# Hi and lo parts of the output projection's operand made earlier and kept in DRAM, in a transformer block's fp32 kernel

## The chip, the cores and the metric

The kernel runs on one core of one Trainium2 chip. The metric is the device time of one execution in microseconds. Engines are named as the profile names them: PE (TensorE matmuls), PEld (its weight loads), DVE (VectorE), ACT (ScalarE), POOL (GpSimd) and SP, whose queue issues most loads.

## The reference, cut to what matters

One block over 512 tokens of width 2048. An input projection feeds two mixers; their outputs are joined, projected and added to the residual; a gated feed-forward layer follows. What the change touches is the joint in the middle:

```python
u = rmsnorm(h, attn_norm_w[l])
z, xbc, dt_raw, q, kc, vc, ks, vs, kw, vw, gate_raw = jnp.split(u @ w_in[l], split_at, axis=-1)
y_ssd = ssd_mixer(z, xbc, dt_raw, ...)      # ends in: rmsnorm(y * jax.nn.silu(z), norm_w)
y_att = nsa_mixer(q, kc, vc, ks, vs, kw, vw, gate_raw, ...)
mixed = jnp.concatenate([y_ssd, y_att], axis=-1)
h = h + mixed @ w_out[l]
```

`y_ssd` and `y_att` are 1024 wide each: eight tiles of 128 channels by 512 tokens each. The norm inside `ssd_mixer` runs over all 1024 channels, so it needs all eight gated tiles before any of them is final.

## The kernel before, in words

Every matmul is done in a split form: an operand a is written as hi + lo, two tiles in a format that PE multiplies fast, and a product is hi·hi + hi·lo + lo·hi, three matmuls (lines 234 to 236). The hi part is a copy on ACT (`a_hi`, L125), the lo part a difference on DVE or POOL (`lo`, L128; L972 where a scale is folded in).

The input projection is a list of 41 units, each 128 output channels by 512 tokens over 16 blocks of 128 of the contraction. `run_unit` runs a unit: it takes its weights in groups of four blocks (256 KB by SP into the ring `raw`, four buffers, L200), splits each group into `whi` and `wlo` (rings of four buffers each) up to three groups ahead, and does three matmuls a block with the operand `U` (tile name u), which holds the hi and lo parts of 16 blocks. All other work is written as Python generators that a small scheduler `sch` steps: each block of a unit is one tick, and a generator says after how many ticks it wants to go on. A unit's result is taken from PSUM by its generator (`ev_...`), and a unit starts only when the one two before it has been taken.

The order of the units is written out by hand: the dt/gates unit, B, C and X of the SSD mixer, the compressed keys, z0 to z3, and then four attention groups g = 0 to 3, each with VS (selected/window values), KS (keys) and two query units, with the z blocks 4 to 7 set between them: z4 and z5 before group 1, z6 before group 2, z7 before group 3. Attention itself is a generator that runs beside the projection and goes on beside the output projection; when the input projection is over, groups 0 and 1 (four tiles of 128 channels) are finished.

`ev_z` makes a gated tile: DVE scales, ACT gates, POOL multiplies by y (read back from DRAM), the tile goes to `gy_d` in DRAM by POOL's queue (L570), its squares are summed in `acc2`, and after z7 `rms_stats` makes the row `row2` of the norm's factors (flag "r2"). A finished attention tile goes to `at_d` (L896) while the operand `U` is still in use, and after that directly into `U`.

The last unit of the input projection is the second query unit of group 3. Ahead of it `pre_ms` starts `ms_in`, which fills blocks 0 to 7 of `U` with the SSD operand: SP loads a tile of `gy_d` into the ring `raw` (L969), POOL multiplies it by `row2`, ACT makes the hi part with the norm's weight folded in, DVE the lo part (L972). Ahead of the first unit of the output projection `pre_out` starts `ma_in`, which does the like for the attention tiles that are ready: SP loads a tile of `at_d` (L985) into the place of the lo part, ACT makes hi, DVE makes lo in place. The first units of the output projection use blocks 0 to 10 or 11 of the operand (the lists `NS`), the rest is added in a later pass.

The compiler layer under the kernel puts the instructions of every engine in an order by a modelled timeline, so the order on an engine is not that of the program text; for PE alone, from the output projection on, it is that of the text (`manual_schedule`). A buffer of a ring is reused when those who read it are done, a store to DRAM among them.

Of the kernel before, what the change touches and what calls it, by code (L numbers as in the profile page):

```python
# [8 lines left out]
F32 = mybir.dt.float32  # L9
F32R = mybir.dt.float32r  # L10
AF = mybir.ActivationFunctionType
ALU = mybir.AluOpType
# [24 lines left out]
C_AN, C_FN, C_LN, C_SN, C_CW, C_CB, C_PE, C_W2 = 0, 16, 32, 48, 56, 104, 116, 148  # L37
# [78 lines left out]
def body(ctx, tc, xT, w_in, w_out, w_gate, w_up, w_down, w1k, w1v, cols, rows, kst, out):  # L116
    nc = tc.nc
    act, dve, pool, pe = nc.scalar, nc.vector, nc.gpsimd, nc.tensor
    sch = Sched()

    def f(ap):
        return ap.bitcast(F32)

    def a_hi(dst, src, scale=1.0):
        act.activation(dst, src, AF.Copy, scale=scale)  # L125

    def lo(eng, dst, src, hi):
        eng.tensor_tensor(dst, src, f(hi), ALU.subtract)  # L128
# [4 lines left out]
    def mul(eng, o, a, b):  # L133
        eng.tensor_tensor(o, a, b, ALU.mult)  # L134

    def add(eng, o, a, b):
        eng.tensor_tensor(o, a, b, ALU.add)  # L137
# [4 lines left out]
    dram = ctx.enter_context(tc.tile_pool(name="dram", bufs=1, space=bass.MemoryType.DRAM))  # L142
# [9 lines left out]
    def ps_t():  # L152
        return ps("t", 2)

    def ps_v():
        return ps("v", 1)

    def ps_m():
        return ps("m", 1)

    gy_d = dram.tile([8, 128, 512], F32, name="gy_d")
    y_d = dram.tile([4, 128, 512], F32, name="y_d")
    at_d = dram.tile([8, 128, 512], F32, name="at_d")
    h1_d = dram.tile([KD, 128, 512], F32, name="h1_d")
    h_d = dram.tile([NJ, 128, 4, 256], F32, name="h_d")
    g_d = dram.tile([NP, 7, 128, 512], F32, name="g_d")
# [3 lines left out]
    def open_pool(name, stack=None, **kw):  # L170
        es = ExitStack()
        pools[name] = (es, es.enter_context(tc.tile_pool(name=name, bufs=1, reuse_waits="tile", **kw)))
        return pools[name][1]
# [19 lines left out]
    raw, hi_t, lo_t = {}, {}, {}  # L193
# [78 lines left out]
    def col(c, n=1):  # L272
        return colc[:, c:c + n]
# [4 lines left out]
    def rms_stats(acc, n, dst, flag, gap=4):  # L278
        nb = acc.shape[1] // 128
        p = ps_m()  # L280
        for i in range(nb):
            pe.matmul(p[:, i:i + 1], acc[:, i * 128:(i + 1) * 128], ones[:, 0:1], start=True, stop=True)
        dve.tensor_scalar(rst[:, 0:nb], p[:, 0:nb], 1.0 / n, EPS, op0=ALU.mult, op1=ALU.add)
        r = rst[:, 4:4 + nb]
        pool.tensor_tensor(r, rst[:, 0:nb], nhalf[:, 0:nb], ALU.pow)
        yield gap
        p = ps_m()
        for i in range(nb):
            pe.transpose(p[:, i * 128:(i + 1) * 128], r[:, i:i + 1].to_broadcast([128, 128]), ident)
        act.activation(dst, p[:, 0:128 * nb], AF.Copy)  # L290
        sch.flags.add(flag)
# [7 lines left out]
    U = up.tile([128, 2, KD, 512], F32R, name="u")  # L299
    wp = open_pool("wp", side="right")  # L300
# [247 lines left out]
    def ev_z(t):  # L548
        def ev(p):
            yield from sch.wait("r1", ("y", t // 4))  # L550
            g, j = divmod(t, 4)
            if g == 0:
                sp = pools["ssd"][1]
                zs = sp.tile([128, 512], F32, tag="zs", name="zs", bufs=2)
                mul(dve, zs, p, rrow)
                act.activation(zs, zs, AF.Silu)
                q = ps_m()
                for i in range(4):
                    pe.transpose(q[:, i * 128:(i + 1) * 128], R["y", g][:, i, j * 128:(j + 1) * 128], ident)
                mul(dve, zs, q, zs)  # L560
            else:
                yield from sch.wait("att")
                sp = pools["att"][1]
                y = sp.tile([128, 512], F32, tag="yz", name="yz", bufs=1)
                nc.sync.dma_start(y, y_d[j])
                zs = sp.tile([128, 512], F32, tag="qs", name="zs", bufs=2)
                mul(dve, zs, p, rrow)
                act.activation(zs, zs, AF.Silu)
                mul(pool, zs, zs, y)
            nc.gpsimd.dma_start(gy_d[t], zs)  # L570
            if t == 0:
                act.activation(acc2, zs, AF.Square)
            else:
                sq = sp.tile([128, 512], F32, tag="sq" if g == 0 else "yz", name="sq", bufs=1)
                act.activation(sq, zs, AF.Square)
                add(pool, acc2, acc2, sq)
            sch.flags.add(("gy", t))
            if t == 7:
                P2["row2"] = sp.tile([128, 512], F32, tag="yz", name="row2", bufs=1)
                sch.add(rms_stats(acc2, 1024, P2["row2"], "r2"))  # L580
        return ev

    P2 = {}

    def ev_kc(g):
        def ev(p):
# [200 lines left out]
    def attention():  # L787
# [6 lines left out]
        for g in range(4):  # L794
# [22 lines left out]
            p = ps_t()  # L817
# [51 lines left out]
            def pvmm(h, br):  # L869
                th, tl = pt.pop((h, br))  # L870
                if br == 0:
                    o = po[h] = ps_v()
                    pe.matmul(o, vpad[:, h, :], ch, start=True, stop=False)
                    pe.matmul(o, vpad[:, h, :], cl, start=False, stop=False)
                o = po[h]
                for kb in range(4):
                    for t in (th, tl):
                        rhs = t[:, 4 * kb:3 * kb + 4, :].rearrange("p a b -> p (a b)")
                        pe.matmul(o[:, kb * 128:512], v[:, kb, br, :], rhs, start=False,
                                  stop=(br == 1 and kb == 3 and t is tl))  # L880
                if br == 1:
                    if h % 2 == 0:
                        R["at"] = ap.tile([128, 512], F32, tag="at", name="at", bufs=1)
                    at = R["at"]
                    a, b = (0, 64) if h % 2 == 0 else (64, 0)
                    fo = ap.tile([128, 512], F32, tag="fo", name="fo", bufs=1)
                    act.activation(fo[a:a + 64, :], o[b:b + 64, :], AF.Copy)
                    add(dve, at[a:a + 64, :], o[a:a + 64, :], fo[a:a + 64, :])
                    if h % 2:
                        k = 2 * g + h // 2  # L890
                        if "ma" in P2:
                            h_, l_ = P2["ma"][k]
                            a_hi(h_, at)
                            lo(dve, l_, at, h_)
                        else:
                            nc.gpsimd.dma_start(at_d[k], at)  # L896
                            P2["at"] = k
                        sch.flags.add(("at", k))

            n = len(items)  # L900
            for s in range(n + LAG + 1):
# [7 lines left out]
                if s < n:  # L909
                    norm(*items[s])  # L910
                yield P2.get("pace", PACE)[s % len(PACE)]
                if 0 <= s - LAG - 1 < n and items[s - LAG - 1][2] == 3:
# [38 lines left out]
        order += [U_B[g], U_C[g]] + U_X[g]  # L951
    order += U_KC + U_Z[0:4]
    for g in range(4):
        z = {0: [], 1: [4, 5], 2: [6], 3: [7]}[g]
        order += [U_Z[t] for t in z] + [U_VS[g], U_KS[g]] + U_Q[g]
    units = [Unit(win(u), KD, u_rhs, ev[u], pre=pre_att if u == U_VS[0] else (lambda: pre_ms()) if u == order[-1] else None) for u in order]


    def pre_ms():
        P2["ms"] = [(U[:, 0, k], U[:, 1, k]) for k in range(8)]  # L960
        sch.add(ms_in())

    def ms_in():
        assert "r2" in sch.flags
        for k in range(8):
            yield 2
            h_, l_ = P2["ms"][k]
            t = wp.tile([128, 512], F32, tag="raw", name="gy", bufs=4)
            nc.sync.dma_start(t, gy_d[k])  # L969
            mul(pool, t, t, P2["row2"])  # L970
            a_hi(h_, t, scale=col(C_SN + k))
            dve.scalar_tensor_tensor(l_, t, col(C_SN + k), f(h_), op0=ALU.mult, op1=ALU.subtract)  # L972
            sch.flags.add(("ms", k))

    def pre_out():
# [5 lines left out]
    def ma_in(n):  # L981

        for k in range(n):
            h_, l_ = P2["ma"][k]
            nc.sync.dma_start(f(l_), at_d[k])  # L985
            yield 1 if k < 4 else 8
            a_hi(h_, f(l_))
            lo(dve, l_, f(l_), h_)
            sch.flags.add(("ma", k))

    def ev_os(c):
        def ev(p):
            if c >= 12:
                t = wp.tile([128, 512], F32, tag="raw", name="h1", bufs=4)
            else:
                t = pools["att"][1].tile([128, 512], F32, tag="yz", name="h1", bufs=1)
            act.activation(t, p, AF.Copy)
            nc.gpsimd.dma_start(t, xT[c], accum_op=ALU.add)
            yield 4
            nc.gpsimd.dma_start(h1_d[c], t)  # L1000
        return ev
# [720 lines left out]
    for v, (j, a, b) in enumerate(visits):  # L1722
# [14 lines left out]
        for n, p in enumerate(SEQ_D):  # L1737
            blk, sums = q["form"][p]
            if n == 0 and v in (2, 4):
                later[5 + (v == 4)] = len(items)  # L1740
            s = Step(blk, g_rhs(p, a), bk(p), after=af(p),
                     before=down_before(v, n) if n < 2 and v < NJ - 1 else None, sums=sums)
# [30 lines left out]
    for k in range(KD):  # L1773
        if k % 4 == 0:
            issue_split(k // 4)
        t = xt[:, k, :]
# [5 lines left out]
    for k in range(KD):  # L1782
        t = xt[:, k, :]
# [125 lines left out]
```

## Time and profile before

| | |
|---|---|
| median of 3 runs | 2241.39 us (2238.38 to 2245.98) |
| the profiled execution | 2243.56 us, span 2241.8 us |
| mean granted clock of PE | 0.986 |
| busy over the span | PE 97%, PEld 85%, DVE 80%, ACT 53%, POOL 19% |
| input projection, first to last matmul | 7.0 to 611.6 us |
| first matmul of the output projection | 631.8 us |
| loads of `gy_d` tiles by SP | 597.8 to 626.2 us |

Times are counted from the start of the span. A row of the timeline gives start, duration, engine, line, operation, output<-input, and in brackets the idle time before it with what ended it. A row of a group gives count, then busy time and mean duration in ns, then the idle time before. A table by stretches gives its length and the busy time (with the number of instructions) of PE, PEld, DVE, ACT and POOL, then PE's granted clock, the share of the DMA engines' time and GB/s. Busy PE is not PE at its peak: the clock in the same row has to be read with it.

### The profile page before, as it was taken

The page shows a single profiled execution, that of the slowest core. Times are in us where ns is not written, and L with a number is a line of the kernel's source. Part 1 is how long each engine was busy: PE and PEld are TensorE (multiplying, and loading weights), DVE is VectorE, ACT ScalarE, POOL GpSimd, SP SyncE. Part 2 cuts the span into 40 slices and gives each one's busy share as a digit, 9 for nine tenths or more (in the row PEclk, how much of TensorE's full clock was granted, in tenths as well). Part 3 has the DMA queues.
Part 4 walks back from the last instruction along what each step waited for, and adds up shares of the span by engine and source line. Part 5 has one row for each costly group of instructions (what it writes and reads, how often), then busy time and mean ns, then how long its engine had stood idle before and what let it go on. Part 6 is the DMA issues. An engine that isn't in the chain of part 4 may idle for free. (4 is left out here: it accounts for less than half of the span.)

```text
span 2241.8 us, 34995 instructions
## 1 busy us (share of the span) xinstructions
PE 2167.7 (97%) x12892; PEld 1908.6 (85%) x12892; DVE 1794.5 (80%) x2821; ACT 1196.4 (53%) x1991; POOL 432.3 (19%) x439
## 2 busy tenths in 40 slices
PE   7999999999999999999999999999999899999996
PEld 5888888888878887888888888888888889999996
DVE  7699766778886648988888888888887878888886
ACT  4564446666666657555555555555555333333453
POOL 2011225234331126000100000000000122221232
PEclk9999999999979999999999999999999999999998
DMA  5222343222334367788888788887878869686974
GB/s 179 90 71 76 120 151 100 76 83 69 97 88 116 104 189 226 223 222 251 227 228 235 219 249 231 239 235 214 249 218 268 315 197 307 191 283 183 298 184 135
DMA packets 170492, 416.66 MB, mean 186 GB/s; under 512 B 16800, under 2 KB 23984, under 8 KB 170320
## 3 DMA queue, kind: packets, MB, share of 16 engines
q1 hardware_dynamic: 98912, 246.73, 33.0%
q0 software_dynamic: 28112, 80.65, 18.4%
q10 hardware_dynamic: 43296, 87.04, 10.8%
q8 instruction: 101, 1.65, 0.3%
q14 instruction: 71, 0.58, 0.1%
HBM read 353.54 MB, written 57.15 MB: 183 GB/s over the span
## 5 line engine op out<-in xcount | busy, mean ns | idle before, releaser
L125 ACT ACTIVATE R<-Z 128x1024 fp32r<-128x1024 f32 (+4 forms) x458 | 415.5, 922 | 438.7 <-DVE Z L137 322.7
L128 DVE TENSOR_TENSOR R<-Z,R 128x1024 fp32r<-128x1024 f32 (+4 forms) x367 | 386.1, 1061 | 35.9 <-ACT R L125 21.1
L234 PE MATMUL ps_g<-u,whi 128*128 128x512 f32 x778 | 316.0, 406 | 0.0
L236 PE MATMUL ps_g<-u,wlo 128*128 128x512 f32 x778 | 307.7, 395 | 0.0
L235 PE MATMUL ps_g<-u,whi 128*128 128x512 f32 x778 | 306.3, 394 | 0.0
L1180 PE MATMUL ps_s<-u,R 128*128 128x512 f32 (+1 forms) x1160 | 252.9, 348 | 7.1 <-ACT A L1390 6.8
L128 DVE TENSOR_TENSOR wlo<-wraw,whi 128x512 fp32r<-128x512 f32 x211 | 159.5, 757 | 80.8 <-ACT whi L125 77.5
L1180 PEld LDWEIGHTS ps_s<-u,R 128*128 128x128 f32 x1160 | 187.7, 188 | 38.7 <-ACT A L1390 12.2
L125 ACT ACTIVATE whi<-wraw 128x512 fp32r<-128x512 f32 x211 | 131.9, 625 | 144.8 <-PE ps_g L235 98.6
L236 PEld LDWEIGHTS ps_g<-u,wlo 128*128 128x128 f32 x778 | 146.6, 188 | 30.6
L234 PEld LDWEIGHTS ps_g<-u,whi 128*128 128x128 f32 x778 | 147.0, 189 | 24.9 <-issue 0.2
L235 PEld LDWEIGHTS ps_g<-u,whi 128*128 128x128 f32 x778 | 147.1, 189 | 23.8
L1180 PE MATMUL ps_t<-u,R 128*128 128x512 f32 (+1 forms) x600 | 131.4, 347 | 0.0
L1180 PE MATMUL ps_g<-u,R 128*128 128x512 f32 x584 | 131.3, 349 | 0.0
L1180 PE MATMUL ps_s<-T,R 128*128 128x512 f32 (+1 forms) x560 | 125.7, 349 | 1.3 <-DVE R L128 1.3
L1180 PE MATMUL ps_g<-T,R 128*128 128x512 f32 (+1 forms) x584 | 125.7, 346 | 0.0
L1180 PE MATMUL ps_s<-V,R 128*128 128x512 f32 (+1 forms) x568 | 123.1, 347 | 0.0
L125 ACT ACTIVATE R<-A 128x1024 fp32r<-128x1024 f32 (+3 forms) x76 | 71.0, 934 | 86.3 <-DVE A L137 62.2
L137 DVE TENSOR_TENSOR Z<-Z 128x1024 f32<-128x1024 f32 (+5 forms) x96 | 106.1, 1105 | 8.8 <-POOL E L137 4.2
L137 DVE TENSOR_TENSOR A<-ps_g,A 128x512 f32<-128x512 f32 (+1 forms) x110 | 71.1, 653 | 51.5 <-PE ps_g L1180 38.6
L128 DVE TENSOR_TENSOR E<-Z,R 128x1024 fp32r<-128x1024 f32 (+1 forms) x91 | 109.9, 1208 | 1.5 <-ACT R L125 1.0
L1180 PEld LDWEIGHTS ps_t<-u,R 128*128 128x128 f32 x600 | 98.0, 188 | 14.1
(487 smaller groups left out, 5621.4 us busy)
## 6 DMA issues: line engine op xcount, KB each, us to landing
Z<-in_w_up SPq DMA_DIRECT2D x94, 512.0 KB, 5.3
Z<-in_w_gate SPq DMA_DIRECT2D x94, 512.0 KB, 6.4
wraw<-in_w_in SPq DMA_DIRECT2D x164, 256.0 KB, 2.5
g_d<-A ACTq DMA_DIRECT2D x22, 1792.0 KB, 15.0
Z<-in_w_up POOLq DMA_DIRECT2D x37, 512.0 KB, 8.9
Z<-in_w_gate POOLq DMA_DIRECT2D x37, 512.0 KB, 7.0
Z<-in_w_down SPq DMA_DIRECT2D x59, 320.0 KB, 5.7
Z<-in_w_down SPq DMA_DIRECT2D x41, 384.0 KB, 4.1
```

Of the source, the lines that this page charges most:

```text
L125: act.activation(dst, src, AF.Copy, scale=scale)
L128: eng.tensor_tensor(dst, src, f(hi), ALU.subtract)
L137: eng.tensor_tensor(o, a, b, ALU.add)
L234: pe.matmul(p, hi_t[i][:, j, :], ah, start=(k == 0), stop=False)
L235: pe.matmul(p, hi_t[i][:, j, :], al, start=False, stop=False)
L236: pe.matmul(p, lo_t[i][:, j, :], ah, start=False, stop=(k == u.nk - 1))
L1180: pe.matmul(o, w, x, start=start, stop=(k == n - 1 and o is q), skip_group_check=not fresh[0])
```

## The change

The hi and lo parts of the SSD operand and of the attention tiles that finish early are made while the input projection still runs, and kept in DRAM as parts: `at_d` gets two tiles for each, a new `gp_d` holds the SSD operand. A helper `parts` makes hi on ACT and lo on DVE in buffers of the rings `whi` and `wlo` and stores both by POOL's queue. A generator `ms_parts`, started by z7's generator, waits for "r2" and then does one tile in ten ticks: load of `gy_d` by SP into the ring `raw`, multiply on POOL, `parts`. Ahead of the last unit `pre_ms` waits (in the scheduler) until the eighth is made; `ms_in` now only loads both parts of a tile, 512 KB, into `U` by SP, and `ma_in` does the same for attention tiles. So that "r2" comes early enough, z5 is moved from group 1 to group 2, and z7 from group 3 to group 2: z4 before group 1; z5, z6 and z7 before group 2; none before group 3.

```diff
-    at_d = dram.tile([8, 128, 512], F32, name="at_d")
+    at_d = dram.tile([8, 2, 128, 512], F32, name="at_d")
+    gp_d = dram.tile([8, 2, 128, 512], F32, name="gp_d")
...
                 sch.add(rms_stats(acc2, 1024, P2["row2"], "r2"))
+                sch.add(ms_parts())
...
+    def parts(dst, t, scale=None):
+        h = wp.tile([128, 512], F32R, tag="whi", name="hp", bufs=4)
+        l = wp.tile([128, 512], F32R, tag="wlo", name="lp", bufs=4)
+        if scale is None:
+            a_hi(h, t)
+            lo(dve, l, t, h)
+        else:
+            a_hi(h, t, scale=scale)
+            dve.scalar_tensor_tensor(l, t, scale, f(h), op0=ALU.mult, op1=ALU.subtract)
+        nc.gpsimd.dma_start(dst[0], f(h))
+        nc.gpsimd.dma_start(dst[1], f(l))
+
+    def ms_parts():
+        yield from sch.wait("r2")
+        for k in range(8):
+            yield 8
+            t = wp.tile([128, 512], F32, tag="raw", name="gy", bufs=4)
+            nc.sync.dma_start(t, gy_d[k])
+            mul(pool, t, t, P2["row2"])
+            yield 2
+            parts(gp_d[k], t, col(C_SN + k))
+            sch.flags.add(("gp", k))
...
-                            nc.gpsimd.dma_start(at_d[k], at)
+                            parts(at_d[k], at)
...
-        z = {0: [], 1: [4, 5], 2: [6], 3: [7]}[g]
+        z = {0: [], 1: [4], 2: [5, 6, 7], 3: []}[g]
...
     def pre_ms():
         P2["ms"] = [(U[:, 0, k], U[:, 1, k]) for k in range(8)]
+        sch.run_until(("gp", 7))
         sch.add(ms_in())
 
     def ms_in():
-        assert "r2" in sch.flags
         for k in range(8):
             yield 2
-            h_, l_ = P2["ms"][k]
-            t = wp.tile([128, 512], F32, tag="raw", name="gy", bufs=4)
-            nc.sync.dma_start(t, gy_d[k])
-            mul(pool, t, t, P2["row2"])
-            a_hi(h_, t, scale=col(C_SN + k))
-            dve.scalar_tensor_tensor(l_, t, col(C_SN + k), f(h_), op0=ALU.mult, op1=ALU.subtract)
+            nc.sync.dma_start(f(U[:, :, k, :]), gp_d[k].rearrange("s p t -> p s t"))
             sch.flags.add(("ms", k))
...
     def ma_in(n):
         for k in range(n):
-            h_, l_ = P2["ma"][k]
-            nc.sync.dma_start(f(l_), at_d[k])
-            yield 1 if k < 4 else 8
-            a_hi(h_, f(l_))
-            lo(dve, l_, f(l_), h_)
+            nc.sync.dma_start(f(U[:, :, 8 + k, :]), at_d[k].rearrange("s p t -> p s t"))
             sch.flags.add(("ma", k))
+            yield 1
```

## The prediction

> **What bounds the kernel now.** I read the page first, then the busy time by stretch around the stage that the change touches, then the instructions of TensorE, VectorE and GpSimd there in order of time.
>
> ```profile
> span 2241.8 us, 34995 instructions
> PE 2167.7 (97%) x12892; PEld 1908.6 (85%) x12892; DVE 1794.5 (80%) x2821; ACT 1196.4 (53%) x1991; POOL 432.3 (19%) x439
> PE   7999999999999999999999999999999899999996
> PEclk9999999999979999999999999999999999999998
> ```
>
> TensorE is the bound nearly everywhere; a gain can come only from a place where it idles or has lost its clock. The one dip of the clock is the twelfth slice (617 to 673 us). That is the handover from the input projection to the output projection, and it is where the change takes its work away.
>
> ```profile
> 487.50:612.50 125.00, 124.53 (x662) 105.51 (x661) 99.04 (x260) 85.80 (x199) 46.10 (x48) 1.00 0.26 83
> 497.50:577.50 80.00, 79.53 (x424) 66.93 (x422) 63.99 (x167) 53.85 (x126) 26.87 (x26) 1.00 0.23 75
> 597.00:631.76 34.76, 29.18 (x141) 25.31 (x140) 32.07 (x64) 24.19 (x53) 24.20 (x24) 0.80 0.39 124
> 612.96:616.16 3.20, 0.00 (x1) 0.00 (x1) 3.20 (x7) 2.16 (x6) 2.65 (x5) 1.00 0.30 75
> 616.16:617.50 1.34, 0.87 (x3) 0.44 (x4) 1.28 (x4) 1.18 (x4) 0.56 (x1) 1.00 0.80 252
> 617.50:631.76 14.26, 12.35 (x52) 11.19 (x53) 14.14 (x25) 8.36 (x18) 10.98 (x10) 0.51 0.27 89
> 631.76:653.40 21.64, 18.96 (x80) 15.11 (x81) 19.16 (x53) 14.33 (x34) 4.70 (x4) 0.77 0.30 86
> ...
> 611.23 0.39 PE L236 MATMUL ps_g<-u,wlo 128*128 128x512 f32 x1
> 616.16 0.50 PE L834 MATMUL ps_s<-kh,rq 128*128 128x512 f32 x1 [3.20 <-DVE em L838]
> 628.75 0.39 PE L776 MATMUL ps_m<-kch,uq 128*128 128x32 f32 x1 [1.23 <-POOL uq L128]
> 631.76 0.77 PE L234 MATMUL ps_g<-u,whi 128*128 128x512 f32 x1
> 643.21 0.49 PE L879 MATMUL ps_v<-pth,v 128*128 128x512 f32 x1 [1.36 <-ACT pth L125]
> ```
>
> The columns of a stretch are its length, then the busy time of PE, PEld, DVE, ACT and POOL, the clock, DMA share and GB/s. Up to 612.5 TensorE lost 0.47 us in 125. The last matmul of the input projection starts at 611.23, the first of the output projection at 631.76; between them run only leftovers of attention and of the last two query blocks. VectorE is busy there without a break (3.20 of 3.20, 14.14 of 14.26), and TensorE waits first for it.
>
> What TensorE lost, and so the most that can come back:
> - up to 631.76: 3.20 idle, 1.34 - 0.87 = 0.47 idle, 14.26 - 12.35 = 1.91 idle, and the clock: 12.35 us of work at 0.51 would take 6.30 at full clock, a loss of 6.05. Together 11.6.
> - 631.76 to 653.40: 21.64 - 18.96 = 2.68 idle and 18.96 x 0.23 = 4.36 of clock: 7.0.
>
> The ceiling is 18.7 us.
>
> **What the change takes out of the handover.**
>
> ```profile
> L972 DVE SCALAR_TENSOR_TENSOR u<-gy,colc,u 128x512 fp32r<-128x512 f32 x8 | 6.5, 825 | 0.9 <-ACT u L125 0.9
> L128 DVE TENSOR_TENSOR u<-u 128x512 fp32r<-128x512 f32 x4 | 3.5, 866 | 0.1
> L134 DVE TENSOR_TENSOR em<-em,gat 128x1 f32<-128x1 f32 x5 | 3.6, 728 | 0.1
> L128 DVE TENSOR_TENSOR rq<-ro,rq 64x512 fp32r<-64x512 f32 x2 | 3.4, 1696 | 0.1
> L134 POOL TENSOR_TENSOR gy<-gy,row 128x512 f32<-128x512 f32 x8 | 11.5, 1445 | 7.2 <-DMA gy<-gy_d 5.7 <-DVE em L838 1.3
> L125 ACT ACTIVATE u<-gy,colc 128x512 fp32r<-128x512 f32 x8 | 5.7, 716 | 3.6 <-POOL gy L134 3.6
> ...
> 602.72 2.56 POOL L134 TENSOR_TENSOR gy<-gy,row 128x512 f32<-128x512 f32 x2
> 602.89 1.14 DVE L134 TENSOR_TENSOR em<-em,gat 128x1 f32<-128x1 f32 x1
> 612.42 1.76 DVE L128 TENSOR_TENSOR wlo<-wraw,whi 128x512 fp32r<-128x512 f32 x1
> 638.02 0.68 DVE L128 TENSOR_TENSOR wlo<-wraw,whi 128x512 fp32r<-128x512 f32 x1
> 639.91 0.16 DVE L134 TENSOR_TENSOR em<-em,gat 128x1 f32<-128x1 f32 x1
> ```
>
> VectorE's own share is 6.5 us for the lo parts of the SSD operand and 3.5 for those of four attention tiles: 10.0. Besides, the GpSimd multiplies that go with them stretch VectorE: a one-element multiply takes 1.14 us beside a multiply of gy and 0.16 without, a weight split 1.76 instead of 0.68. The five one-element multiplies of the group take 3.6 instead of 0.8 (2.8), the split 1.08 more, the two rq differences, at 1.70 each beside two GpSimd operations of which one is a multiply of gy, 1.0, and I add 1.0 for the rest: an estimated 5.9. So 16 of the 32.07 us of VectorE between 597 and 631.76 go. ScalarE loses 5.7 and four copies, which bounded nothing.
>
> By the Trainium skill, "SBUF — State Buffer", section "Who interferes with whom", a GpSimd operation and a VectorE one with two SBUF inputs exclude each other for a whole instruction; the trace agrees (1.14 against 0.16).
>
> How far the start of the output projection then comes forward depends on what is late next:
>
> ```profile
> 611.24 0.67 DVE L134 TENSOR_TENSOR qt<-ps_g,rrow 128x512 f32<-128x512 f32 x1
> 623.60 1.27 ACT L125 ACTIVATE uq<-qt 64x512 fp32r<-64x512 f32 x2
> 627.38 1.32 POOL L128 TENSOR_TENSOR uq<-qt,uq 64x512 fp32r<-64x512 f32 x1
> ```
>
> The last query block needs qt (611.24 to 611.91), its hi copies (1.27) and two GpSimd differences of 1.3 before its score matmuls: without queues, about 616. Now ScalarE reaches it only at 623.60, behind exponentials that wait for VectorE. TensorE has work to fill the time until then: the 0.87 + 6.30 us counted above, so about 620 at the earliest by TensorE's own work (631.76 - 11.6). By VectorE: 32.07 - 16 = 16 us of work after 597 plus the gaps that stay, so about 616, later by whatever it is behind when it gets there. I take 622.5: 9.3 of the 11.6. Below nothing the term can hardly go, as nothing is added on VectorE there but one lo part of the last finished attention tile (0.7).
>
> Of the second part's 7.0 I take 2.5: the wait of 1.36 and the slow clock just after 631.76 go if VectorE is no longer behind, the rest belongs to the start of the next attention group, which is unchanged. Ends: 0 and 7.0.
>
> **What it adds before.**
>
> ```profile
> L134 DVE TENSOR_TENSOR zs<-ps_g,rrow x4: 680/682/692, 370.8 to 547.4; 128x512 f32<-128x512 f32 x4
> L290 ACT ACTIVATE row<-ps_m x1: 577/577/577, 562.1 to 562.1; 128x512 f32<-128x512 f32 x1
> L570 POOL DMA_DIRECT2D gy_d<-zs x8: 544/584/629, 263.1 to 551.6; - x8
> L896 POOL DMA_DIRECT2D at_d<-at x4: 586/590/618, 443.7 to 619.8; - x4
> ACT whi L125 <- PE ps_g L235: 13.4, 13, 2.7
> ```
>
> From the first of these z blocks to the last, eleven units, it is 370.8 to 547.4: 16 us a unit, 1.0 us a block of the contraction (a tick). The last is gated at 547.4 and the row of the norm is there at 562.1. The change moves that block four units earlier, so the row is there near 498, and the eight parts, ten ticks apart, fall into 498 to 578. The number of ticks up to the end of the projection is unchanged, so attention has the same steps in it; and the wait for the last part ahead of the last unit finds it made (some 90 ticks needed, 112 there).
>
> - VectorE: 63.99 of 80 now, plus 8 x 0.75 = 6.0, two attention lo parts at an estimated 0.7 (0.87 beside the stretching) and the stretching of 5.9, less one z gating (0.68): 76.6 of 80. Nearly full, not over; before and after it has room (in 487.5 to 612.5 it works 99 of 125). TensorE needs only the weight splits of it at once, attention can lag.
> - GpSimd: 26.87 of 80, plus 8 multiplies of 1.3 and 18 more store issues of 0.59: 48. The queries' rotations queue behind these; they are needed a unit or more later.
> - ScalarE: 53.85 of 80, plus 5.7 and two copies: 61.
> - Weight buffers: the parts sit in the rings of the split weights (four each) until both stores have landed. Making (0.7 + 0.75), two issues and 2.5 to land hold one slot of four some 6 us out of every 10. ScalarE already waits 13.4 us for such a slot in 440 to 700; the split is then two weight groups (of four ticks) ahead of TensorE instead of three: 8 us.
>
> Cost on TensorE: at the low end 0 (0.47 lost now), at the high end 5.9 (all the stretching paid by TensorE). I take 1.0, near the low end, since 76.6 still fits. By the lock rule of "SBUF — State Buffer" in the Trainium skill, taken at its word, each of the eight multiplies blocks VectorE for its whole 1.28: 10.2 instead of 5.9, 81 of 80, and the sum below would be about one us less.
>
> **The loads that take their place.**
>
> ```profile
> gy<-gy_d SPq DMA_DIRECT2D x8, 256.0 KB, 2.6
> u<-at_d SPq DMA_DIRECT2D x4, 256.0 KB, 2.7
> gy_d<-zs POOLq DMA_DIRECT2D x8, 256.0 KB, 2.5
> Z<-in_w_up SPq DMA_DIRECT2D x94, 512.0 KB, 5.3
> ```
>
> Twelve loads of 512 KB replace twelve of 256, now straight into the operand. Each must wait on SP's queue until the last unit has read that block (16 blocks that end at 611.6, so some 597 to 604 for the first eight), and weight loads queue behind it; those for the first blocks were issued before. 4.2 MB at the 252 GB/s that the row of 616.16 shows is 17 us: landed by about 616, four more by 624, used from 622 on at 1.0 us a block, the attention tiles from the ninth. I cost it at 0; if the first matmul had to wait for a load issued late, 5.3.
>
> **Sum.** -9.3 - 2.5 + 1.0 = -10.8 us. The profiled execution took 2243.56 us (span 2241.8), 2.2 over the median of the runs, 2241.39. Against its own time that is 2232.8, against the median 2230.6, say 2231. Nothing behind 653 is changed in kind: TensorE is full there, so what is won is kept.
>
> **Rivals.**
> - More comes back (gain 14 to 18.7; about 2225): VectorE, freed of 16 us, lets the clock stay at full through 653. For it: one stall of 3.20 us started the slow stretch. Against: attention's new group starts there with VectorE at 19.16 of 21.64.
> - The debt is carried over (gain 0 to 6.7; about 2238): VectorE, nearly full from 498 to 578, reaches 612 with attention behind, a stall remains and the clock falls again. For it: 76.6 of 80 leaves no room for waits in its queue. Against: 26 us of idle VectorE in 487.5 to 612.5. By the Trainium skill, "TensorE: Matmul & The Clock Gate", Part 1, an idle window of about 3.4 us halves the clock and as much activity restores it: the loss would be 1.7, not 6.05, and the removed stall would bring some 4.4 less (sum -6.4). The row of 14.26 us at 0.51 says otherwise here, where work comes in small pieces.
> - Slower: the slots. A part whose stores queue on GpSimd behind a query block's GpSimd work holds its slot beyond 10 us; then two of four slots are gone, the next group's split starts only when TensorE ends the group before it, and TensorE waits a copy, a difference and their queues, about 2.5 us. All eight so: 20 lost against 11.8 gained, about 2249. From five parts in eight on it decides. Against: GpSimd at 48 of 80 has room.
> - The loads come late (gain about 5): counted with the debt.
>
> **Chances.** Forecast (gain 6.7 to 14) 0.48, more 0.15, debt or late loads 0.24, slots 0.13. 0.3% (6.7 us) is about what a measurement can tell from no change here: faster 0.63, same 0.25, slower 0.12 (a little of the slots' case ends within it). The range goes from the ceiling, 2223, to 2243, which leaves out the slots' case.
>
> **What would show it.** The first output-projection matmul near 622 and a clock near 1.0 in 612 to 632; VectorE below full there; the wait of 3.20 gone. Eight part makings between 498 and 578 with TensorE full. Wrong if TensorE waits for wlo or whi in 498 to 578, for the loads of u after 612, or if the stall before the score matmuls and the clock of 0.5 are still there.

## The result, and the profile after

The changed kernel is slower: 2254.75 us (median of 7 runs, 2250.64 to 2261.5) against 2244.06 us for the kernel before beside it (7 runs, 2238.38 to 2247.11). The ratio is 1.0052, with a 95% interval of 1.0034 to 1.0069, so 8 to 15 us more. Forecast were 11 us less.

The head of the page after:

```profile
span 2252.9 us, 35045 instructions
PE 2173.9 (96%) x12892; PEld 1912.3 (85%) x12892; DVE 1788.6 (79%) x2821; ACT 1195.1 (53%) x1991; POOL 438.8 (19%) x459
PE   7999999999989999999999999999999899999996
```

The page in 40 slices hardly shows the loss: the one digit of TensorE's row that changed is the twelfth (619.6 to 675.9 us), which now holds the handover. Shorter stretches show it. Busy time by stretch, first of after, then one row of before; the columns are those of the prediction's table (length, PE, PEld, DVE, ACT, POOL, clock, DMA share, GB/s):

```profile
487.50:612.50 125.00, 116.70 (x584) 96.06 (x583) 92.34 (x242) 74.61 (x180) 52.94 (x61) 0.95 0.34 110
512.50:562.50 50.00, 45.72 (x214) 36.86 (x213) 36.41 (x79) 28.36 (x66) 29.48 (x35) 0.93 0.44 139
601.45:621.90 20.45, 15.39 (x64) 12.04 (x62) 15.60 (x51) 15.34 (x42) 2.88 (x3) 0.75 0.00 0
638.18:647.62 9.44, 6.81 (x45) 6.34 (x43) 2.82 (x8) 3.88 (x9) 8.05 (x9) 0.89 1.05 371
```

```profile
512.50:562.50 50.00, 49.52 (x274) 41.92 (x273) 40.58 (x107) 33.82 (x79) 19.47 (x18) 1.00 0.22 71
```

In 487.5 to 612.5 TensorE now loses 8.3 us and some clock (0.95); before it lost 0.47. VectorE is *less* busy there than before (92 against 99 of 125): it isn't overloaded, TensorE has run out of something. The stretch from 601.45 to 621.90 holds no projection matmul at all. The handover itself did shrink: the stretch without projection matmuls was 20.53 us (611.23 to 631.76) and is 9.44 (638.18 to 647.62), and VectorE works 2.82 us of it. It only starts 27 us later.

What TensorE ran out of is split weights. Two places of ScalarE's timeline of after, in order of time; the rows left out at "..." hold no split of a weight:

```profile
480.52 0.63 ACT L125 ACTIVATE whi<-wraw 128x512 fp32r<-128x512 f32 x1 [2.08 <-issue]
...
500.60 0.64 ACT L125 ACTIVATE hp<-at 128x512 fp32r<-128x512 f32 x1
501.12 1.67 ACT L125 ACTIVATE whi<-wraw 128x512 fp32r<-128x512 f32 x3
```

```profile
591.35 0.63 ACT L125 ACTIVATE whi<-wraw 128x512 fp32r<-128x512 f32 x1 [1.00 <-DVE ptl L128]
...
618.30 0.59 ACT L912 ACTIVATE fo<-ps_v 64x512 f32<-64x512 f32 x1 [1.16 <-PE ps_v L904]
...
620.70 0.63 ACT L125 ACTIVATE hp<-at 128x512 fp32r<-128x512 f32 x1
621.22 1.67 ACT L125 ACTIVATE whi<-wraw 128x512 fp32r<-128x512 f32 x3
```

How long SP's queue waited for a weight buffer (total, times, longest), after and before:

```profile
SPq L201 <- DVE wlo L128: 93.3, 25, 29.8
```

```profile
SPq L200 <- DVE wlo L128: 94.3, 26, 7.7
```

Before, this wait is as long in sum, but never over 7.7 us. After, no weight is split from 480.52 to 501.12 and from 591.35 to 621.22, and each of these pauses ends within 0.6 us of the start of the hi part of an attention tile (`hp<-at`), which itself starts within 3 us of the copy `fo` that finishes the tile. Three splits then follow at once: their raw weights were there already. Before, the longest pause of the splits between 440 and 610 is 7.1 us.

One more correction, to the prediction and to what stands ahead of it. The input projection's 37 units that use ps_g have 37 x 48 = 1776 matmuls; up to 611.23 the trace of before has 594 on each of the three lines, 1782, and the program's order on TensorE has the same six more ahead of the last score matmuls. So 611.23 is not the last matmul of the input projection but the sixth of the output projection: two blocks of it already ran, and 631.76 is its third block. This matters below.

### The profile page after: what moved, and what is told of

It reads as the page before. It is cut to its first block, busy times and chain, and to the rows that moved or that the text cites. A ratio compares the mean times of both kernels' runs of the same rounds, so it can differ in the third digit from the quotient of the medians.

```text
span 2252.9 us, 35045 instructions
## 1 busy us (share of the span) xinstructions
PE 2173.9 (96%) x12892; PEld 1912.3 (85%) x12892; DVE 1788.6 (79%) x2821; ACT 1195.1 (53%) x1991; POOL 438.8 (19%) x459
## 3 DMA queue, kind: packets, MB, share of 16 engines
q10 hardware_dynamic: 43296, 87.04, 10.8%
```

## The experiments

The theories, when the result was known:
- **A, the order of the slots.** A ring hands out its buffers in the order in which the text asks for them. A part that is asked for before its data exists holds back every weight split asked for after it.
- **S, the prediction's slots.** A part holds its slot too long *after* it is made, since its stores queue on GpSimd.
- **B, the work.** The added multiplies and parts, and what they do to VectorE, cost TensorE 500 to 580.
- **C, the order of the z blocks** costs by itself.

All ratios are to the kernel before on the same chip. A good summary of each trace is the start of the last matmul of the three-matmul split form on the line of hi x lo weights (the end of the output projection's first pass), here for before, after, and the six kernels that matter most (the four attention tiles alone in the rings; no part in the rings; only the SSD parts in the rings; attention parts asked for later; and the two with TensorE's order freed, without and with ready parts):

```profile
L236 PE MATMUL ps_g<-u,wlo x778: 387/391/628, 69.1 to 823.0; 128*128 128x512 f32 x195
```

```profile
L237 PE MATMUL ps_g<-u,wlo x778: 387/389/628, 70.1 to 835.4; 128*128 128x512 f32 x195
```

```profile
L236 PE MATMUL ps_g<-u,wlo x778: 387/390/628, 69.4 to 832.8; 128*128 128x512 f32 x195
```

```profile
L237 PE MATMUL ps_g<-u,wlo x778: 387/392/628, 69.0 to 817.5; 128*128 128x512 f32 x195
```

```profile
L237 PE MATMUL ps_g<-u,wlo x778: 387/392/628, 69.4 to 823.6; 128*128 128x512 f32 x195
```

```profile
L237 PE MATMUL ps_g<-u,wlo x778: 387/389/628, 70.2 to 819.3; 128*128 128x512 f32 x195
```

```profile
L236 PE MATMUL ps_g<-u,wlo x778: 387/390/628, 70.2 to 823.1; 128*128 128x512 f32 x195
```

```profile
L237 PE MATMUL ps_g<-u,wlo x778: 387/392/628, 69.9 to 814.2; 128*128 128x512 f32 x195
```

What each gained or lost by 823.0, in the one execution that was profiled (+12.4, +9.8, -5.5, +0.6, -3.7, +0.1, -8.8), is within about 2 us of its whole gain or loss by the ratio (for the four attention tiles alone, 4.6 us): little is made or lost behind that point.

**Only the z blocks moved** (kernel before, with the other order).

```diff
-        z = {0: [], 1: [4, 5], 2: [6], 3: [7]}[g]
+        z = {0: [], 1: [4], 2: [5, 6, 7], 3: []}[g]
```

> The kernel before with only the z blocks moved (z4 before group 1, z5 to z7 before group 2). Theory A (the parts take buffers of the weight rings; a ring is handed out in the order of the program, so the splits of weights behind a part in the program wait for that part): no change against before, within 4 us of 2244, first output-projection matmul within 4 us of 631.8. Theory B (the parts' work on VectorE and GpSimd is too much for the projection): no change either. Theory C (the moved z blocks themselves disturb the order): about +10 us, first output-projection matmul near 647.

Measured: 1.0001 (0.9988 to 1.0013). C falls; the move is free, as forecast.

**After, with the attention tiles handled as before** (one store of the whole tile, hi and lo made behind the load).

```diff
-                            parts(at_d[k], at)
+                            nc.gpsimd.dma_start(at_d[k], at)
...
```

> The changed kernel with the attention tiles handled as before (whole tiles in DRAM, split when loaded); only the SSD operand's parts are made early. Theory A: the gap in weight splits between 591 and 621 us behind the last early attention tile goes, the last unit's matmuls run before about 615; the loss in 500 to 575 (about 11 us) stays; total near 2244, first output-projection matmul between 625 and 640. Theory B: four copies and four differences less in the projection change little, total 2250 to 2254.

Measured: 1.0005 (0.9992 to 1.0018). The loss is gone, and that between 500 and 575, which was expected to stay, nearly went with it: TensorE is busy 78.78 of 80 us in 497.5 to 577.5, against 75.15 in after. The eight parts of the SSD operand, with their multiplies, loads and stores, cost next to nothing, but bring nothing either: a stretch of 23.5 us (615.37 to 638.86) has no projection matmuls, more than before.

**The reverse: the kernel before, with only the attention tiles as parts.**

```diff
-                            nc.gpsimd.dma_start(at_d[k], at)
+                            parts(at_d[k], at)
...
```

> The kernel before with only the early attention tiles kept as parts, made in the weight rings; SSD operand and z blocks as before. Theory A: the splits behind the last early attention tile wait for it (it is ready near 617), so 10 to 20 us without projection matmuls before the last unit, total 2248 to 2256. Theory B (load of the parts' work): four copies and differences more beside the projection and as many less behind it, total within 3 us of before.

Measured: 1.0064 (1.0049 to 1.0078), 14 us slower by four tiles alone. From its stretches and ScalarE's timeline:

```profile
591.74:607.97 16.23, 11.82 (x66) 8.47 (x64) 14.41 (x46) 14.15 (x38) 2.83 (x3) 1.00 0.00 1
```

```profile
576.16 0.63 ACT L125 ACTIVATE whi<-wraw 128x512 fp32r<-128x512 f32 x1 [1.55 <-PE ps_g L235]
...
606.76 0.63 ACT L125 ACTIVATE hp<-at 128x512 fp32r<-128x512 f32 x1
607.29 1.67 ACT L125 ACTIVATE whi<-wraw 128x512 fp32r<-128x512 f32 x3
```

Again a pause of 31 us in the splits that ends with the tile, and 16 us without a projection matmul.

**After, with the parts in buffers of their own** (one each for hi, lo and the tile of gy; the rings cut from four to three to make room), **and the kernel before with the rings cut alike.**

```diff
-        h = wp.tile([128, 512], F32R, tag="whi", name="hp", bufs=4)
-        l = wp.tile([128, 512], F32R, tag="wlo", name="lp", bufs=4)
+        h = wp.tile([128, 512], F32R, tag="hp", name="hp", bufs=1)
+        l = wp.tile([128, 512], F32R, tag="lp", name="lp", bufs=1)
...
-LEAD = 3
+LEAD = 2
...
```

> The changed kernel with parts in buffers of their own (one for hi, one for lo, one for the gy tile), taken from the rings, which go from four buffers to three, with the split two groups ahead instead of three. Same work on every engine as in the changed kernel. Theory A: weight splits come evenly, no gap over 10 us, TensorE full from 500 to 600, first output-projection matmul near 622 plus what three buffers cost by themselves (see the control), total 2232 to 2238 if that is nothing. Theory B: total stays near 2254.

> Control: the kernel before with rings of three buffers and the split two groups ahead, nothing else. Every theory: 0 to +6 us against before (the weight split has about 2.7 us a group and needs some 1.4); it says what of the run with buffers of their own is the shorter ring.

Measured: 0.9992 (0.9979 to 1.0005) and, for the control, 1.0008 (0.9996 to 1.0021). The splits are even again: no pause over 8.5 us between 440 and 610. With three buffers, the difference of the two is 0.0016, some 3.6 us in favour of the parts, though the two intervals overlap. That is less than theory A had allowed for (2232 to 2238; measured 2243.08).

**After, no part in the rings, four buffers kept**: hi has one buffer of its own, lo takes the place of the whole tile (room is made by moving small SSD tiles into a pool that is closed by then).

```diff
-        h = wp.tile([128, 512], F32R, tag="whi", name="hp", bufs=4)
-        l = wp.tile([128, 512], F32R, tag="wlo", name="lp", bufs=4)
+        h = wp.tile([128, 512], F32R, tag="hp", name="hp", bufs=1)
+        l = t.bitcast(F32R)
...
```

> The changed kernel with the rings left at four buffers and two groups-ahead unchanged (three), but the parts out of the rings whi and wlo: hi in one buffer of its own, lo made in place of the whole tile. Room for it comes from small SSD tiles and a row of constants that move to the pool closed before attention. The gy tiles stay in the ring raw. Theory A (order of the rings whi and wlo): splits even, no gap over 10 us, last projection matmul before 618, total 2238 to 2243 (the run with buffers of its own stood 5 us under its control of shorter rings). If the ring raw (weight loads behind gy loads) is what couples: gaps as in the changed kernel between 500 and 575, total near 2250.

Measured: 0.9976 (0.9964 to 0.9988): 2237.63 against 2244.45, faster than both kernels. The work on the engines is that of after; the place of the parts turns +11.7 us into -5.4.

**Only the attention parts out of the rings**, the SSD parts left in.

```diff
-        h = wp.tile([128, 512], F32R, tag="whi", name="hp", bufs=4)
-        l = wp.tile([128, 512], F32R, tag="wlo", name="lp", bufs=4)
+        if scale is None:
+            h = wp.tile([128, 512], F32R, tag="hp", name="hp", bufs=1)
+            l = t.bitcast(F32R)
+        else:
+            h = wp.tile([128, 512], F32R, tag="whi", name="hp", bufs=4)
+            l = wp.tile([128, 512], F32R, tag="wlo", name="lp", bufs=4)
...
```

> The changed kernel with only the attention tiles' parts taken out of the rings of the split weights; the eight parts of the SSD operand stay in them. Theory A, as shown with the attention tiles alone (13 us for four of them in the rings): what couples is a part whose data hangs on lagging attention. The parts of the SSD operand have data that is ready (one load and one multiply), so they should cost 0 to 4 us against the version with no part in the rings: 2238 to 2242. If any part in the rings costs as much as another (eight against four), it is 2250 or more.

Measured: 0.9993 (0.9979 to 1.0006). Eight SSD parts in the rings cost about 0.0017 (4 us; the two intervals overlap), the four attention parts another 0.0059 (13 us). It is not the number of parts but whether their data is there when the slot comes up.

**After, with the attention parts asked for later**, same rings, same stores: this tells A from S.

```diff
+                        def place(k=k, at=at):
+                            if "ma" not in P2:
+                                yield (28 if k == 3 else 44)
...
+                                parts(at_d[k], at)
...
+                        sch.add(place())
```

> The changed kernel with one difference: the parts of a finished attention tile are asked for 44 ticks later in the text (28 for the fourth), still in the rings of the split weights and with the same stores. In ScalarE's built order the fourth tile's hi part then stands behind the 119th split of the weights instead of the 107th (124th in the version with no part in the rings). Theory A (a slot asked for by the text ahead of its data holds all later splits back until attention has made the data): the splits come evenly again, no gap of over 12 us in them up to 615, and the time returns to that with only the SSD operand's parts in the rings, 2242 to 2248. Rival S (a part holds its slot while its stores queue on GpSimd): the stores are the same, so the time stays at 2252 to 2257.

Measured: 0.9983 (0.997 to 0.9996): 2239.54 against 2244.51. A stands, and S falls as the cause of the loss: the slots and the stores are the same, only the place in the text at which the slot is asked for has moved, and 15 us are back, a little more than expected. The trace of after says the same of S. Two rows of GpSimd's timeline there:

```profile
545.79 0.61 POOL L596 DMA_DIRECT2D gp_d<-hp  x1
...
621.63 0.60 POOL L596 DMA_DIRECT2D at_d<-hp  x1 [15.05 <-ACT hp L125]
```

The last row is the store of the fourth attention tile's hi part. GpSimd had been idle for 15.05 us and waited for the part, and the splits were running again (621.22) before the store was even issued: they had waited for the part to be made, not for its stores. From start to landing the hi parts of the four attention tiles held a slot for 3.3 to 4.6 us. S may have played a part once: the first row is the store of an SSD part made by 539.81, which stood behind work for the queries and landed at 548.32. The next part began at 548.38, but its own multiply had ended only at 548.27, so the trace does not tell which of the two it waited for; TensorE ran no projection matmul from 545.49 to 552.97.

How the place in the text becomes a place in time is seen in the order on ScalarE. Counted in the timelines, the number of weight splits (`whi<-wraw`) ahead of the last two copies of group 1 and of the fourth tile's hi part:

```
kernel before        fo | splits ahead 162     fo | splits ahead 168
after                fo | splits ahead 159     fo | splits ahead 159     hp<-at | splits ahead 159
no part in the rings fo | splits ahead 162     fo | splits ahead 168     hp<-at | splits ahead 168
asked for later      fo | splits ahead 162     fo | splits ahead 166     hp<-at | splits ahead 166
```

(The counts 107, 119 and 124 in the expectations do not match the timelines, nor do their distances; their order does.) The input projection has 41 x 4 = 164 splits, at four blocks each. Before, all of them and four more stood ahead of the end of group 1. After, the 160th had to wait for it, and with it the last five groups of the input projection.

**The work itself**: no part in the rings, and the eight GpSimd multiplies by the norm's row left out.

```diff
-            mul(pool, t, t, P2["row2"])
             yield 2
             parts(gp_d[k], t, col(C_SN + k))
...
```

> The version with the parts outside the rings, and the eight multiplies of the SSD operand by the norm's row on GpSimd left out (the operand then lacks that factor). Theory B (the stretched VectorE instructions cost TensorE in 500 to 580, estimated at 5.9 us of VectorE and 1.0 of time): 0.5 to 2 us faster than with them, about 2236. If VectorE's lost time passes through in full, 5 us, about 2232; if it is hidden, 2237.6.

Measured: 0.9972 (0.9957 to 0.9986), against 0.9976 with them. As the cause of the 11.7 us B had fallen before, since the version with no part in the rings does the same work and loses nothing. This run adds that what the multiplies do to VectorE costs no time that can be measured here: the difference is 0.9 us, and the two intervals overlap so far that the 0.5 to 2 us that B still allowed are neither shown nor excluded.

**Why the gain stops at 5 us: two buffers for the queries' stacked parts** (uq), with rings of three, first without and then with the parts made ahead.

```diff
-        ap.tile([128, 2, 512], F32R, tag="uq", name="uq", bufs=1)
+        ap.tile([128, 2, 512], F32R, tag="uq", name="uq", bufs=2)
...
```

> The kernel before with rings of three buffers (the control) and two buffers for uq, the query operand of the compressed scores. It tests what sets the length of the handover (control: 615.1 to 635.8). If it is VectorE's load, as the prediction had it: no change against the control, handover 20 us. If it is the chain (values' transposes, then one PSUM bank, then the first block's score matmuls, then the single uq buffer, then GpSimd, then the second block's): uq of the last block is made near 617 instead of 625, handover 13 to 16 us, total 4 to 7 us under the control.

> Parts out of the rings whi and wlo (as in hp1), rings of three buffers, two buffers for uq. If VectorE's load and the uq chain both hold the handover, this is the shortest of all: handover under 12 us, total 2232 to 2238. If the chain alone holds it: as the run with two uq buffers, near 2241.

Measured: 1.0045 (1.0031 to 1.0058) and 0.9988 (0.9978 to 0.9998). The last block's uq was ready early (616.62 and 615.24 on ScalarE), but the stretch without projection matmuls stayed: 21.3 us, and 17.3 with the parts, against 20.8 and 17.0 with one buffer. This buffer does not set the handover. Without the parts, the second buffer makes the kernel slower than its control (1.0045 against 1.0008, 8 us); why stays open.

**Why the gain stops: TensorE's order.** From the first unit of the output projection on, the order on TensorE is that of the text. There, two blocks of the output projection are followed by what attention has left at that point and by the score matmuls of the last query block, and the third block may not pass them. Moving the start of the fixed order by two units lets the modelled order place 10 to 17 blocks ahead (by the program's order, six matmuls before, and 52, 42 and 31 in the three kernels below).

```diff
-NU = 41
+NU = 43
```

> The version with the parts outside the rings of the split weights, and TensorE's order kept by the text only from the third unit of the output projection on (before: from the first). In the built order of every kernel so far two blocks (six matmuls) of the output projection stand ahead of the last score sets, and the third block behind them; here twelve blocks stand ahead. Theory H (what is left of the handover is this fixed order: TensorE may not take the third block before the score matmuls of the last query block, whose operand comes late): the stretch without projection matmuls of 17.8 us (612.04 to 629.88) breaks up, 612.5 to 637.5 shows TensorE at 23 or more of 25 with the clock over 0.85 instead of 21.05 at 0.73, and the time falls by 4 to 8 us below the version with the fixed order, to about 2230 to 2234. Rival V (VectorE's attention work sets it): the blocks are taken early, TensorE then idles as long behind them, and the time stays within 2 us of 2237.6.

> The kernel before with the order of TensorE kept by the text only from the third unit of the output projection on. Theory H: part of the 18.7 us of the handover comes back without any parts made ahead, but the third and later blocks now wait for their own hi and lo parts, which VectorE and ScalarE make in 597 to 632, so less than with the parts ready: 2 to 5 us, about 2240. If the gain is as large as the one beside the ready parts, the parts bring nothing of their own at this place; if there is none, it is VectorE that sets the handover before.

> The changed kernel with TensorE's order kept by the text only from the third unit of the output projection on. In ScalarE's built order the fourth tile's hi part still stands behind the 107th split. Theory A: the time lost by 600 stays, and the freer order can give back only a part of what the handover still costs (9.4 us without projection matmuls there): 2250 to 2256. If the fixed order is the whole reason for the loss, it falls to 2240 or less.

Measured: with no part in the rings 0.9956 (0.9943 to 0.9969), 2236.85 against 2246.46, the lowest ratio of all (its interval overlaps that of 0.9976 a little); the kernel before 0.9998 (0.9986 to 1.001); the changed kernel 1.0028 (1.0016 to 1.004), so some 5 of its 11.7 us hang on the order and the rest stays. The stretch 612.50 to 637.50, in the version with no part in the rings, the same with the freed order, and the kernel before with the freed order:

```profile
612.50:637.50 25.00, 21.05 (x94) 17.66 (x93) 18.43 (x47) 11.73 (x30) 10.77 (x12) 0.73 0.46 157
```

```profile
612.50:637.50 25.00, 24.70 (x143) 21.09 (x142) 20.49 (x50) 14.86 (x38) 12.75 (x14) 1.00 0.79 256
```

```profile
612.50:637.50 25.00, 19.69 (x102) 15.54 (x100) 24.65 (x48) 15.51 (x37) 17.89 (x17) 0.90 0.36 116
```

In the handover, ready parts and the freed order go together. With both, TensorE is busy 24.70 of 25 us at full clock; the freed order without ready parts leaves VectorE busy without a break (24.65 of 25) and gains nothing; ready parts without the freed order leave VectorE room (18.43) and TensorE waiting for its turn. By the ratios, 4.5 of the forecast 10.8 us sat behind an order that the change didn't touch. A part of what the freed order wins in the stretch is paid back right behind it, where attention, pushed back, runs without projection matmuls (642.37 to 657.05):

```profile
637.50:662.50 25.00, 21.16 (x113) 16.74 (x113) 22.21 (x74) 18.93 (x51) 1.45 (x2) 1.00 0.19 52
```

## Why the prediction was wrong, point by point

- **Weight buffers: the step that failed.** It priced a part by how long it stays in a slot once made, "some 6 us out of every 10", and concluded that splits would be two weight groups ahead instead of three. It never asked when the part's data would come, and applied the price of the SSD parts to the attention tiles, of which it counted only the lo parts on VectorE and the copies on ScalarE. The runs: the fourth tile's slot, asked for in the text at its turn, kept all later splits back from 591.35 until the tile was made at 620.70. The sign that the prediction named for this showed as well: in 498 to 578 TensorE waited 1.3 us for wlo and 0.7 us for whi. The term "cost on TensorE" was 1.0, with 5.9 as its upper end; the rings cost 17 us (from 1.0052 to 0.9976), about 13 of them for the attention tiles. (The terms given for the holding time add up to 5.1, not 6; in after the SSD parts held a slot for 3.4 to 10.5 us. That size was not what failed.)
- **The rival "slots"** had the right resource and sign and came nearest in time (2249), but by another mechanism: it hung on GpSimd's queue, and what spoke against it was that "GpSimd at 48 of 80 has room". GpSimd did have room (29.48 of 50 in the stretch above). Of the twelve parts one had its stores held up there as the rival says (at 545.79); the long pauses came from attention. That the time is near is luck.
- **Attention can lag.** The prediction used this as a reserve ("attention can lag"). That was true before, where no split had to wait for an attention tile's slot. The change tied the two together and took the reserve away.
- **The start of the output projection, 622.5: mechanism right, size off.** VectorE's work in the handover did go. The stretch without projection matmuls, before and in the version with no part in the rings:

```profile
611.23:631.76 20.53, 14.95 (x66) 13.04 (x65) 20.35 (x38) 12.43 (x28) 15.92 (x16) 0.66 0.32 100
```

```profile
612.04:629.88 17.84, 13.89 (x69) 11.92 (x68) 12.49 (x31) 8.76 (x23) 11.18 (x12) 0.76 0.62 216
```

  VectorE falls from 20.35 to 12.49 us, but the start comes at 629.88, not 622.5: 1.9 of the 9.3 us of that term. The step took TensorE's own work and VectorE as the only bounds; the fixed order behind the score matmuls was a third one. With it moved, and with no part in the rings, the 11 us of the sum come nearly out: 9.9 by the ratio.
- **The clock.** In the version with no part in the rings the prediction's dip stays:

```profile
620.00:626.00 6.00, 5.65 (x28) 5.48 (x28) 5.87 (x13) 2.13 (x5) 3.91 (x4) 0.60 0.40 138
626.00:632.00 6.00, 5.12 (x20) 4.73 (x21) 2.30 (x7) 0.91 (x4) 2.09 (x2) 0.50 0.06 24
```

  TensorE is over 85% busy there, most of it with small matmuls, and the clock stays low for 12 us. By the Trainium skill, "TensorE: Matmul & The Clock Gate", Part 1, some 3.4 us of activity restore it; these rows do not agree, as the row of 14.26 us at 0.51 did not before. From 626.88 on TensorE worked without a wait, and the clock was still 0.50 in 632 to 634; it rose in 634 to 636 (0.79), some 5 us after the first projection matmul at 629.88. Whether small matmuls count as activity no run here shows.

  The second term (2.5, behind 631.76) came, and was rather larger. Before, and with no part in the rings, the idle time and the clock's loss in these 25 us are 2.68 + 3.12 = 5.8 and 1.35 us:

```profile
637.50:662.50 25.00, 22.32 (x107) 18.19 (x106) 19.95 (x66) 18.30 (x46) 1.52 (x2) 0.86 0.26 75
```

```profile
637.50:662.50 25.00, 23.65 (x131) 19.97 (x130) 19.15 (x64) 20.45 (x52) 2.39 (x3) 1.00 0.31 83
```
- **The parts' times: right but for some 10 us.** Forecast 498 to 578, seen 509.1 to 587.6 for the eight hi parts, with the stalls:

```profile
L125 ACT ACTIVATE hp<-gy,colc x8: 710/724/728, 509.1 to 587.6; 128x512 fp32r<-128x512 f32 x8
```

- **VectorE nearly full in 498 to 578, and the stretching by multiplies: harmless.** The lock that the prediction cites from the Trainium skill ("SBUF — State Buffer", "Who interferes with whom") may well hold VectorE: in the version with no part in the rings its busy time in 487.5 to 612.5 falls from 105.02 to 100.09 us without the eight multiplies, near the estimated 5.9. But leaving them out moved the time by less than can be measured. The rule would have made 10.2 us of it on VectorE, and no run shows any of it in the time.
- **The loads: cost 0, right.** They take longer than the row of before let expect (8.0 and 9.8 us to landing, medians, against the 5.3 of a 512 KB load), and TensorE waited for none of them. Its waits from 612 to 700 in after name no operand u:

```profile
PE ps_t L888 <- DVE em L872: 2.7, 2, 1.5
PE ps_m L801 <- POOL uq L128: 2.6, 2, 2.3
PE ps_g L237 <- DVE wlo L128: 0.7, 1, 0.7
PE ps_s L859 <- DVE em L863: 0.3, 1, 0.3
```

What stays open: whether the SSD parts in the rings cost 4 us and why (with them alone in the rings a pause of 10.2 us in the splits, 549.95 to 560.12, ends 0.6 us after the start of an SSD part's hi, 559.51, which fits A, but the intervals overlap), and whether the attention that the freed order pushes back to 642 could be spread without loss.

## What to carry to other kernels

When work of another chain borrows buffers from the ring that feeds the critical engine, ask not how long it holds a buffer, but when its data comes relative to its turn: in a ring filled in the order of the text, one late guest stops every later tenant, however idle the engines are. Give it a buffer of its own, or ask for the ring's slot only when the data is sure to be there. And before counting on time freed at a place, look at the order on the engine that is to use it: what stands next in its queue may wait for something that the change does not touch.

## What the runs showed of the hardware that was not expected

- Loads of 512 KB issued close together ran at 371 GB/s in the 9.44 us from 638.18, together with loads of weights, against 252 GB/s in the best stretch that the prediction shows, but took 8.0 and 9.8 us to land (medians) instead of 5.3: the time of a transfer read where the queues are quiet does not hold in a burst.
- A granted clock of 0.60 and 0.50 in two rows of 6 us went with a TensorE that was over 85% busy and no wait of TensorE over 1.5 us in 611 to 632, whereas with projection matmuls filled in between it did not fall (1.00 in 612.50 to 637.50).
